# One layer of a hybrid decoder on one core: the last pair's forms moved into the second Strassen product, first loads on another queue, and result rows in another order

## The chip, the core and the metric

The kernel runs on one core of a Trainium2 chip. The core has a matrix engine (TensorE, PE in the profile, with its weight loads as PEld), a vector engine (VectorE, DVE), a scalar engine for activations (ScalarE, ACT), a general engine (GpSimd, POOL) and a queue engine that issues transfers (SyncE, SP). Sixteen DMA engines move data between the main memory and the on-chip memory (SBUF); matmul results go to eight banks of PSUM. All engines run on their own and wait for each other by semaphores. The metric is the device time of one execution in microseconds, here the median of three runs.

## The reference, cut to what matters

One layer for 1024 prompt positions and 8 single new positions, 1032 rows, width 1024, all in float32:

```
x = x + concat(gdn_heads(x), gating_heads(x)) @ w_out
x = x + square(relu(rms_norm(x, g_ff) @ w_up)) @ w_down        # 1024 -> 4096 -> 1024
x = x + (p @ w_ple) * sigmoid(rms_norm(x, g_ple) @ w_ple_gate) # p is 256 wide
y = rms_norm(x, g_final)
```

The change touches the second line's `w_down` product and how it begins, and the third and fourth lines.

## The kernel before

Float32 matmuls are made of three: every operand is split into a high part (a rounded copy, made by ScalarE) and a low part (the rest, made by VectorE), and hi*hi, lo*hi and hi*lo are summed in PSUM. Weights are split by `form` (lines 150 and 153), with four splits in flight.

Activations lie transposed, model columns on the partitions and rows on the free axis. The 1032 rows stand in four blocks of 256, 256, 260, 260; in the last stages they are two halves `nn` of two column blocks each, so a block number n has nn = n % 2 and column block n // 2. `q` numbers the 128-row output blocks of a half: q 0 and 1 lie in column block 0, q 2, 3 and 4 (the last with four rows) in column block 1.

Both products of the MLP use Strassen's scheme in the form with seven products, P1 to P7, in place of eight. In the first (lines 1167 to 1219) `p` counts 16 pairs of hidden units, t the two column blocks; the inputs' seven forms lie in `fb` and `fa` (fa serves P1, P4, P5; fb the others). Each pair's four results lie in one buffer `Q`; ScalarE copies P1's and P6's products out of PSUM, VectorE adds the others, ScalarE does relu and square in two passes, and `dforms` makes three subtractions on GpSimd (four of the seven forms that the second product needs) and writes three planes from Q and four from `tt` to `f_d` in main memory. For the last pair, relu and square of two planes are one VectorE instruction (line 1210), and its writes are issued by GpSimd. `up_rows` is a thread of extra work on the residual rows `x1_d` that takes one step per pair and column block.

In the second product (`down`, lines 1434 to 1507) four groups j of the hidden units each run the seven steps P1, P6, P7, P4, P2, P5, P3; n counts these 28 steps. Step n needs one plane of `f_d` in `raw` (`load_raw`), split into HC (`split_raw`: line 1347 on ScalarE, 1348 on VectorE, two halves each), and four forms of weights: P1 takes A11 alone, P6 the sums s1 = A21 + A22 and s2 = s1 - A11 (GpSimd, lines 1368 and 1369), P7 and P3 differences (line 1375). Each step has 96 matmuls on four parts p and two column blocks, and VectorE adds each result into one or two accumulators (lines 1463 and 1465): ACC holds C11, C12, C21, C22, and U2 and U3 lie beside it. `x1_old` loads the residual into an accumulator before the step that first adds to it. PE's and SP's orders are those of the program here; other engines' orders are chosen by the scheduler from priorities and readiness.

The on-chip memory is reused in place: xs, h1, A12, A22, A21, h0, A11 and raw take the space of fb, fa and Q. A22 lies under the end of fb, and A11, raw and h0 lie under fa. Later xt, wpl and pp take the space of h1, A12, A22, A21, h0 and A11.

In the last stage `gate_units` makes 8 x 4 gate products (24 matmuls each, lines 1658 to 1660) with the embedding product (`emb`, six matmuls), and `evg` multiplies by the row factor, takes a sigmoid, multiplies and adds to ACC (line 1649). Blocks 0 and 2 (half 0) come first for all m, then 1 and 3. `y_out` turns one 128-row block: two groups of four transposes (line 1626), a square with its sum for each (line 1627), the root of the mean square, two products (line 1636) and two writes (line 1637). The first half's `y_out` run beside the second half's gates; the second half's five come after the last gate. `pt` is the prompt's p, scaled on GpSimd (line 1504) and transposed by `p_in` (line 1579) at the beginning of the gates.

## Time and profile before

| | |
|---|---|
| median of 3 runs | 1414.2 us (1411.84, 1414.2, 1420.41) |
| profiled execution, its own time | 1418.24 us |
| its span, first to last instruction | 1416.5 us |
| PE busy | 1317.7 us, 93% of the span |
| DVE, POOL, ACT busy | 920.8, 696.9, 639.4 us |

The busy times say little by themselves: PE is nearly always busy, so what counts is where it stands, and for whom. The chain of work that ended last gives PE 72% of the span, DVE 9%, POOL 7%, ACT 4% and DMA 3%. PE's waits between 900 and 1270 us are 12.3 us for low parts of weights (DVE, line 153), 6.8 us for high parts (ACT, line 150) and 1.6 us for a copy of the row factor; from 1270 on they are 10.3 us, all for line 1636. The prediction's rows are from the timeline (start, length, engine, line, operation, out<-in, shape, count, and in brackets the idle time before it with what ended it) and from windows, whose columns it names.

### The profile page before, as it was taken

The page shows a single profiled execution, that of the slowest core. Times are in us where ns is not written, and L with a number is a line of the kernel's source. Part 1 is how long each engine was busy: PE and PEld are TensorE (multiplying, and loading weights), DVE is VectorE, ACT ScalarE, POOL GpSimd, SP SyncE. Part 2 cuts the span into 40 slices and gives each one's busy share as a digit, 9 for nine tenths or more (in the row PEclk, how much of TensorE's full clock was granted, in tenths as well). Part 3 has the DMA queues.
Part 4 walks back from the last instruction along what each step waited for, and adds up shares of the span by engine and source line. Part 5 has one row for each costly group of instructions (what it writes and reads, how often), then busy time and mean ns, then how long its engine had stood idle before and what let it go on. Part 6 is the DMA issues. An engine that isn't in the chain of part 4 may idle for free.

```text
span 1416.5 us, 26668 instructions
## 1 busy us (share of the span) xinstructions
PE 1317.7 (93%) x10189; PEld 1286.1 (91%) x10189; DVE 920.8 (65%) x1900; ACT 639.4 (45%) x1346; POOL 696.9 (49%) x720
## 2 busy tenths in 40 slices
PE   6979978999999799899999999789999999999995
PEld 5879968988989799899999999789999999899984
DVE  7745745455956856655545544678878878887664
ACT  6574645532232415555545445424333333545332
POOL 5300888746525404658856777640526136635110
PEclk9999988999999899999999999989999999999997
DMA  7334535545524831234545565776362524232221
GB/s 238 97 91 115 154 81 152 170 126 168 149 83 133 262 96 45 60 119 133 162 144 161 168 195 158 241 258 214 116 221 97 186 85 148 61 91 75 75 91 61
DMA packets 212076, 194.01 MB, mean 137 GB/s; under 512 B 20952, under 2 KB 181659, under 8 KB 211940
## 3 DMA queue, kind: packets, MB, share of 16 engines
q1 hardware_dynamic: 211436, 190.45, 43.6%
q8 instruction: 80, 1.31, 0.4%
q0 software_dynamic: 512, 1.85, 0.3%
q14 instruction: 48, 0.39, 0.1%
HBM read 131.75 MB, written 60.61 MB: 136 GB/s over the span
## 4 chain that ended last, share of the span: by engine, by line
PE 72%; DVE 9%; POOL 7%; ACT 4%; DMA 3%; issue 3%; SPq 1%; DVEq 0%; ACTq 0%; POOLq 0%
PE A L1184 9%; PE d L1457 7%; PE d L1458 7%; PE d L1456 7%; PE D L1184 7%; PE g L209 5%; PE g L211 5%; PE g L210 5%; PE B L1184 3%; PE C L1184 3%; PE g L1658 2%; POOL it L643 2%; POOL xinv L644 2%; PE g L1660 2%; PE g L1659 2%
## 5 line engine op out<-in xcount | busy, mean ns | idle before, releaser
L209 PE MATMUL g<-ra,whi 128*128 128x384 f32 (+3 forms) x800 | 275.4, 344 | 0.8 <-ACT ra L388 0.6
L1457 PE MATMUL d<-h,wlo 128*128 128x260 f32 (+1 forms) x896 | 256.7, 286 | 12.3 <-DVE wlo L153 12.3
L1456 PE MATMUL d<-h,whi 128*128 128x260 f32 (+1 forms) x896 | 254.4, 284 | 6.8 <-ACT whi L150 6.8
L211 PE MATMUL g<-ra,whi 128*128 128x384 f32 (+3 forms) x800 | 258.7, 323 | 0.8 <-POOL ra L389 0.4
L210 PE MATMUL g<-ra,wlo 128*128 128x384 f32 (+3 forms) x800 | 257.6, 322 | 0.0
L1458 PE MATMUL d<-h,whi 128*128 128x260 f32 (+1 forms) x896 | 256.0, 286 | 0.0
L1457 PEld LDWEIGHTS d<-h,wlo 128*128 128x128 f32 x896 | 171.4, 191 | 14.3 <-DVE wlo L153 14.0
L1456 PEld LDWEIGHTS d<-h,whi 128*128 128x128 f32 x896 | 172.1, 192 | 7.5 <-ACT whi L150 7.4
L1458 PEld LDWEIGHTS d<-h,whi 128*128 128x128 f32 x896 | 171.8, 192 | 0.0
L209 PEld LDWEIGHTS g<-ra,whi 128*128 128x128 f32 x800 | 156.6, 196 | 3.0 <-ACT ra L388 1.0
L211 PEld LDWEIGHTS g<-ra,whi 128*128 128x128 f32 x800 | 155.8, 195 | 2.5 <-POOL ra L389 1.7
L210 PEld LDWEIGHTS g<-ra,wlo 128*128 128x128 f32 x800 | 156.7, 196 | 0.7 <-DVE wlo L153 0.3
L153 DVE TENSOR_TENSOR wlo<-s,whi 128x512 fp32r<-128x512 f32 x96 | 73.5, 768 | 81.7 <-ACT whi L150 81.4
L153 DVE TENSOR_TENSOR wlo<-st,whi 128x512 fp32r<-128x512 f32 x94 | 75.8, 807 | 40.8 <-ACT whi L150 40.1
L1184 PE MATMUL A<-fb,whi 128*128 128x260 f32 (+1 forms) x512 | 95.6, 281 | 0.0
L643 POOL TENSOR_TENSOR it<-ainv,xinv 32x31 f32<-32x31 f32 (+15 forms) x124 | 75.3, 607 | 39.6 <-DMA ainv<-inv_d 30.3
L150 ACT CAST whi<-s 128x512 fp32r<-128x512 f32 x96 | 59.3, 618 | 76.1 <-PE D L1184 28.5
L1465 DVE TENSOR_TENSOR acc<-acc,d 128x256 f32<-128x256 f32 (+1 forms) x192 | 75.2, 414 | 20.9 <-PE d L1458 19.9
L1347 ACT CAST h<-raw 128x1024 fp32r<-128x1024 f32 (+1 forms) x56 | 58.6, 1055 | 65.2 <-DMA raw<-f_d 35.0
L150 ACT CAST whi<-st 128x512 fp32r<-128x512 f32 x96 | 59.1, 619 | 60.8 <-PE g L211 31.6
L1214 ACT ACTIVATE q<-q 128x512 f32<-128x512 f32 (+1 forms) x124 | 75.9, 631 | 22.0 <-DVE q L1207 16.1
L644 POOL TENSOR_TENSOR xinv<-xinv,it 32x31 f32<-32x31 f32 (+15 forms) x124 | 79.0, 637 | 9.6
(433 smaller groups left out, 3539.9 us busy)
## 6 DMA issues: line engine op xcount, KB each, us to landing
a<-in_w_down SPq DMA_DIRECT2D x16, 1024.0 KB
raw<-f_d SPq DMA_DIRECT2D x28, 520.0 KB
raw<-f_d SPq DMA_DIRECT2D x28, 512.0 KB
st<-in_w_in SPq DMA_DIRECT2D x24, 512.0 KB
ck<-ck_d SPq DMA_DIRECT2D x32, 320.0 KB
ra<-in_w_up SPq DMA_DIRECT2D x32, 256.0 KB
rb<-in_w_up SPq DMA_DIRECT2D x32, 256.0 KB
st<-in_w_ple_gate SPq DMA_DIRECT2D x16, 512.0 KB
```

Of the source, the lines that this page charges most:

```text
L150: S.copy(dst_hi, src)
L153: lo_eng.tensor_sub(dst_lo, src, f32(dst_hi))
L209: PE.matmul(ps[:, :w], lhsT=whi[k], rhs=xh, start=(k == 0), stop=False)
L210: PE.matmul(ps[:, :w], lhsT=wlo[k], rhs=xh, start=False, stop=False)
L211: PE.matmul(ps[:, :w], lhsT=whi[k], rhs=xl, start=False, stop=(k == nk - 1))
L643: G.tensor_mul(tv, a, x)
L644: G.tensor_sub(X[:, j + 1 :, :w], X[:, j + 1 :, :w], tv)
L1184: PE.matmul(ps, lhsT=a[:, k, :], rhs=x[:, c, k, :], start=(first and k == 0 and j == 0), stop=(k == 3 and j == 2), skip_group_check=True)
L1214: placed["act"] = S.activation(v, v, func).ins
L1456: PE.matmul(ps, lhsT=wh[:, k, :], rhs=xh[:, k, :], start=(k == 0), stop=False)
L1457: PE.matmul(ps, lhsT=wl[:, k, :], rhs=xh[:, k, :], start=False, stop=False)
L1458: PE.matmul(ps, lhsT=wh[:, k, :], rhs=xl[:, k, :], start=False, stop=(k == 3))
```

## The change

It has five parts. The last pair's relu and square of two planes and its subtractions leave the end of the first product: they are done in the second step of the second product (n = 1), the squares on ScalarE in two passes, the subtractions into space inside C22, and the four writes are issued by SP after step n = 2. So that they live that long, Q is allocated below fb and fa, and C22's residual is loaded after step 3, not 1. The first raw plane and A11 are loaded on ScalarE's queue, right after that engine's copy of the last pair's P6. `up_rows` takes the first column block of every second m together with the second, four steps fewer.

`pt` moves from the middle of the second product to its end, into space of A22, with its scaling.

In the last stage each half of a result block is multiplied by g_final unscaled, straight after its transposes, and its sum of squares is kept; one root serves several blocks (five in the first half, then three, then two), and the scaling by the root follows: 512 columns on ScalarE, 512 on GpSimd, and for the last two blocks the second half still by line 1636's instruction from PSUM. In the second half block 3 goes before block 1, and of m = 6 and 7 both of block 3 go before those of block 1, so that rows q 2, 3 and 4 are ready first; the table for the square root is loaded early by a dummy activation.

```diff
+        qst = ctx.enter_context(pool("qst"))
+        Q = qst.tile([P, 8 * 260], F32, name="q8")
         fx = ExitStack()
...
-                        S.copy(u2[t], ps)
+                        placed["u2", t] = S.copy(u2[t], ps).ins
...
                 if p == 15 and name == "P3":
-                    v = q[:, 0:4:3]
-                    V.scalar_tensor_tensor(v, in0=v, scalar=0.0, in1=v, op0=ALU.max, op1=ALU.mult)
+                    last.append((p, t, q))
...
+    def squared(v):
+        for func in (AF.Relu, AF.Square):
+            placed["act"] = S.activation(v, v, func).ins
+    def dforms_of(t, q, tt):
+        G.tensor_sub(tt[:, 1:4:2], q[:, 3:4].to_broadcast([P, 2, WT[t]]), q[:, 0:3:2])
+        G.tensor_sub(tt[:, 2], q[:, 2], tt[:, 1])
+        placed["pool"] = G.tensor_sub(tt[:, 0], q[:, 1], tt[:, 2]).ins
+    def dforms_out(p, t, q, tt):
+        w = WT[t]
         c0 = 1024 * t + w * (p % 4)
-        (G if p == 15 else SY).dma_start(f_d[p // 4, 0:3, ...], q[:, 0:3])
-        (G if p == 15 else SY).dma_start(f_d[p // 4, 3:7, ...], tt)
+        SY.dma_start(f_d[p // 4, 0:3, ...], q[:, 0:3])
+        SY.dma_start(f_d[p // 4, 3:7, ...], tt)
...
-                yield
+                if t or m % 2:
+                    yield
...
+    late = [C22.rearrange("p a b -> p (a b)")[:, 1024 * t : 1024 * t + 4 * WT[t]]... for t in range(2)]
...
+                if n:
+                    SY.dma_start(raw[:, c], f_d[j, DSTEPS[i][1], :, c])
+                else:
+                    with tc.issue_after(placed["u2", 0]), tc.high_priority(2 * PRI):
+                        S.dma_start(raw[:, c], f_d[j, DSTEPS[i][1], :, c])
...
+            if j or name != "A11":
+                SY.dma_start(dst, src[:, :, half * 512 : half * 512 + 512])
+            else:
+                with tc.issue_after(placed["u2", 0]), tc.high_priority(2 * PRI):
+                    S.dma_start(dst, src[:, :, half * 512 : half * 512 + 512])
...
+                if n == 1 and p < 2:
+                    _, t, q = last[p]
+                    with tc.issue_after(placed["cast", 1]):
+                        squared(q[:, 0:4:3])
+                    with tc.issue_after(placed["sum"]):
+                        dforms_of(t, q, late[t])
...
+            elif n == 2:
+                for p, t, q in last:
+                    dforms_out(p, t, q, late[t])
+            elif n == 3:
                 x1_old(C22, 1, 1)
-            elif n == 10:
-                SY.dma_start(pt, p_prompt[0, 0].rearrange("(c p) d -> p c d", p=P))
...
+    with tc.high_priority(3 * PRI):
+        SY.dma_start(pt, p_prompt[0, 0].rearrange("(c p) d -> p c d", p=P))
...
+    yot = [Q[:, :1024], Q[:, 1024:2048]] + [ty.tile([P, D], F32, name=f"yo{i}") for i in range(3)]
...
+    def y_half(nn, q, a, keep=False):
+        r = rows_of(q)
+        ps = pss.tile([P, 512], F32, tag="s2", name="yT")
+        for j in range(4):
+            PE.transpose(ps[:r, j * P : j * P + P], ACC[:, a, nn, j, q * P : q * P + r], ident)
+        junk = tp.tile([P, 512], F32, tag="jk", bufs=1, name="jk")
+        S.activation(junk[:r], ps[:r], AF.Square, accum_out=sty[:r, nn, q, a : a + 1])
+        b = slice(512 * a, 512 * a + 512)
+        if not keep:
+            V.tensor_mul(yos[nn, q][:r, b], ps[:r], gfb[:r, b])
+        return ps
+    def y_roots(nn, q0, q1, fast=False):
+        v = rsy[:, nn, q0:q1]
+        V.tensor_add(v, sty[:, nn, q0:q1, 0], sty[:, nn, q0:q1, 1])
+        V.scalar_tensor_tensor(v, in0=v, scalar=1.0 / D, in1=ems[:, nn, q0:q1], op0=ALU.mult, op1=ALU.add)
+        (rsqrt_act if fast else rsqrt)(tp, v, v, f"ry{nn}{q0}")
+    def y_end(nn, q, ps=None):
...
+        S.activation(yo[:r, :512], yo[:r, :512], AF.Copy, scale=s)
+        if ps is None:
+            G.tensor_scalar_mul(yo[:r, 512:], yo[:r, 512:], s)
+        else:
+            V.scalar_tensor_tensor(yo[:r, 512:], in0=ps[:r], scalar=s, in1=gfb[:r, 512:], op0=ALU.mult, op1=ALU.mult)
+        for b in (slice(0, 512), slice(512, 1024)):
             SY.dma_start(y[:, b], yo[:r, b])
...
-        weave(gate_units((1, 3), True))
+        weave(gate_units([(m, n) for m in range(6) for n in (3, 1)], True))
+        spawn(first_halves())
+        weave(gate_units([(6, 3), (7, 3)], True))
+        spawn(second_out(), 2.5)
+        weave(gate_units([(6, 1), (7, 1)], True))
+        with tc.issue_after(placed["sig"]):
+            S.activation(rsy[:, 1, 0:1], ones[:, 0:1], AF.Sqrt)
         drain()
-        for q in range(5):
-            for _ in y_out(1, q):
-                pass
+        pa = [y_half(1, q, 1, True) for q in range(2)]
+        y_roots(1, 0, 2, True)
+        for q in range(2):
+            y_end(1, q, pa[q])
```

`first_halves` runs `y_half(1, q, 0)` for q = 2, 3, 4, 0, 1; `second_out` runs `y_half(1, q, 1)` for q = 2, 3, 4, one root for the three, and their `y_end`.

More of the change, by code (lines that the diff above doesn't have):

```diff
@@ L1318, in trunk_step_kernel @@
     U2, U3 = (dac.tile([P, 4, 516], F32, name=f"u{i}") for i in (2, 3))
+    late = [C22.rearrange("p a b -> p (a b)")[:, 1024 * t : 1024 * t + 4 * WT[t]].rearrange("p (a b) -> p a b", a=4)
+            for t in range(2)]
     INTO = {"P1": (U2, C11), "P6": (U2,), "P7": (U3,), "P4": (C21,), "P2": (C11,), "P5": (C12, C22), "P3": (C12,)}
@@ L1339, in load_raw @@
             for c in (slice(0, 1024), slice(1024, 2064)):
-                SY.dma_start(raw[:, c], f_d[j, DSTEPS[i][1], :, c])
+                if n:
[3 more added lines that the diff above has]
+                        S.dma_start(raw[:, c], f_d[j, DSTEPS[i][1], :, c])
     def split_raw(n):
@@ L1346, in split_raw @@
                 for c in (slice(0, 1024), slice(1024, 2064)):
-                    S.copy(hi[:, c], raw[:, c])
+                    placed["cast", n] = S.copy(hi[:, c], raw[:, c]).ins
                     V.tensor_sub(lo[:, c], raw[:, c], f32(hi[:, c]))
@@ L1368, in down_forms @@
                             G.tensor_add(s1[:, p], a_of("A21", p), a_of("A22", p))
-                            G.tensor_sub(s2[:, p], s1[:, p], a_of("A11", p))
+                            placed["sum"] = G.tensor_sub(s2[:, p], s1[:, p], a_of("A11", p)).ins
                             f = s2[:, p]
@@ L1604, in emb @@
         return ps
-    def root(tok, tag, fast):
-        (rsqrt_act if fast else rsqrt)(tp, tok, tok, tag)
     def rows(nn):
@@ L1614, in rows @@
         arrived("r", nn)
[L1616 to L1636 removed]
+    yos = {(nn, q): yot[q] for nn in range(2) for q in range(5)}
@@ L1637, in y_out, with gate_units @@
             SY.dma_start(y[:, b], yo[:r, b])
-    def gate_units(blocks, last):
-        for m in range(KD):
+    had = {}
+    def gate_units(turns, last):
+        for m, n in turns:
             def evg(ps, n, m=m):
@@ L1649, in evg @@
                 (V if last and m > 5 else G).tensor_add(xv, xv, t)
[L1651 to L1667 removed]
+            if m not in had:
+                had[m] = next_w()
+            ws = had[m]
+            w = WT[n // 2]
+            ps = gps[0].tile([P, 512], F32, tag="g", name="g")[:, :w]
+            for k in (4, 5, 6, 7, 0, 1, 2, 3):
+                wh, wl = (h[:, k % 4, :] for h in ws[k // 4])
+                xh, xl = (h[:, k % 4, TOFF[n // 2] : TOFF[n // 2] + w] for h in XS[k // 4, n % 2])
+                PE.matmul(ps, lhsT=wh, rhs=xh, start=(k == 4), stop=False)
+                PE.matmul(ps, lhsT=wl, rhs=xh, start=False, stop=False)
+                PE.matmul(ps, lhsT=wh, rhs=xl, start=False, stop=(k == 3))
+                if k == 3:
+                    with tc.high_priority(PRI):
+                        if there >= {("p", n % 2), ("r", n % 2)}:
+                            evg(ps, n)
+                        else:
+                            held.append((n, lambda ps=ps, n=n, evg=evg: evg(ps, n)))
+                yield 3 * w * 0.000455
     held, there = [], {("r", 0)}
@@ L1696, in first_out, with first_halves, second_out @@
         for q in range(5):
-            yield from y_out(0, q)
+            for a in range(2):
+                y_half(0, q, a)
+                yield YT
+        y_roots(0, 0, 5)
+        for q in range(5):
+            y_end(0, q)
+    def first_halves():
+        for q in (2, 3, 4, 0, 1):
+            y_half(1, q, 0)
+            yield YT
+    def second_out():
+        for q in (2, 3, 4):
+            y_half(1, q, 1)
+            yield YT
+        y_roots(1, 2, 5)
+        for q in (2, 3, 4):
+            y_end(1, q)
     with tc.manual_schedule(engines={mybir.EngineType.PE}):
```

85 lines of the change are left out of this document (27 added, 58 removed).

## The prediction

> **What bounds the kernel now.** I read the spans first, then the waits of TensorE, then stage windows, then the timelines of the two stretches that the change touches: the hand-over from the first Strassen product (line 1184) to the second (lines 1456 to 1458), and the end.
>
> ```profile
> core 0: 1416.5 us, clock 0.964
> ```
> ```profile
> 913.00:921.50 8.50, 0.57 (x3) 0.19 (x1) 8.24 (x6) 2.52 (x5) 8.29 (x8) 0.67 1.05 386
> 921.50:926.00 4.50, 4.45 (x20) 4.45 (x21) 4.50 (x2) 0.00 (x0) 4.16 (x5) 0.50 1.05 399
> ```
> ```profile
> 935.00:940.00 5.00, 0.32 (x3) 0.11 (x1) 5.00 (x10) 0.62 (x1) 1.79 (x2) 0.98 0.14 32
> 940.00:945.00 5.00, 4.84 (x29) 4.84 (x30) 3.35 (x6) 1.57 (x2) 0.00 (x0) 0.68 0.88 300
> ```
> The columns are the stretch and its length, then busy time (and instructions) of PE, PEld, DVE, ACT, POOL, then granted clock, DMA share, GB/s. Elsewhere PE is full; here it stands for most of 13.5 us, while DVE is full, and in 921.5:926 it runs at half clock (0.50).
>
> ```profile
> 921.55 0.58 PE L1457 MATMUL d<-h,wlo 128*128 128x256 f32 x1 [5.52 <-DVE wlo L153]
> ...
> 940.16 0.58 PE L1457 MATMUL d<-h,wlo 128*128 128x256 f32 x1 [4.84 <-DVE wlo L153]
> ```
> ```profile
> 913.23 0.43 DVE L1207 TENSOR_TENSOR q<-u,D 128x260 f32<-128x260 f32 x1 [0.30 <-PE D L1184]
> 913.69 1.29 DVE L1210 SCALAR_TENSOR_TENSOR q<-q 128x520 f32<-128x520 f32 x1
> 914.90 5.45 DVE L1348 TENSOR_TENSOR h<-raw,h 128x1024 fp32r<-128x1024 f32 x2
> 920.28 9.48 DVE L153 TENSOR_TENSOR wlo<-a,whi 128x512 fp32r<-128x512 f32 x4
> ...
> 937.14 2.37 DVE L1348 TENSOR_TENSOR h<-raw,h 128x1024 fp32r<-128x1024 f32 x2
> 939.43 1.88 DVE L153 TENSOR_TENSOR wlo<-s,whi 128x512 fp32r<-128x512 f32 x3
> ```
> The same DVE work takes 5.45 us at 914.9 and 2.37 at 937.1 (two halves of the low part), 2.37 and 0.63 us each (the weights' low part). The slow ones stand where POOL is full (8.29 of 8.50), the fast ones where it is idle. So the hand-over is bound by DVE slowed beside POOL, and what POOL does first is the last pair's forms (lines 1226 to 1231); the sums for the second step come behind them:
>
> ```profile
> 923.54 5.07 POOL L1368 TENSOR_TENSOR s<-a,a 128x512 f32<-128x512 f32 x4
> 930.49 1.32 POOL L1375 TENSOR_TENSOR sd<-a,a 128x512 f32<-128x512 f32 x1 [1.88 <-issue]
> 931.75 5.03 POOL L1369 TENSOR_TENSOR s<-s,a 128x512 f32<-128x512 f32 x4
> 949.55 1.30 POOL L1375 TENSOR_TENSOR sd<-a,a 128x512 f32<-128x512 f32 x1 [12.76 <-DVE wlo L153]
> ```
> The end: five blocks of result rows after the last gate matmul (1393.63 + 0.28 = 1393.9) take to 1416.5, 22.6 us, a chain of transposes, squares, a root and a product for each block, with two buffers.
>
> ```profile
> 1393.63 0.28 PE L1603 MATMUL em<-pp,wpl 128*128 128x260 f32 x1
> ```
> ```profile
> 1394.60 0.43 DVE L1649 TENSOR_TENSOR acc<-acc,t 128x260 f32<-128x260 f32 x1
> 1395.82 0.16 DVE L1630 TENSOR_TENSOR st<-st 128x1 f32<-128x1 f32 x1 [0.79 <-ACT yo L1627]
> 1396.01 0.16 DVE L1631 SCALAR_TENSOR_TENSOR st<-st,ems 128x1 f32<-128x1 f32 x1
> ```
> ```profile
> 1396.38 1.28 ACT L261 ACT_TABLE_LOAD   x1
> ```
> ```profile
> 1412.63 0.73 DVE L1636 SCALAR_TENSOR_TENSOR yo<-yT,st,gfb 4x512 f32<-4x512 f32 x1
> 1412.73 0.93 SPq L1637 DMA_DIRECT2D out<-yo  x2
> ```
>
> **Part 1: hand-over.** Removed from it: the two products of line 1210 on DVE, six POOL subtractions, four POOL DMAs. Moved before it: the loads of raw and A11.
>
> ```profile
> 903.28 0.37 ACT L1198 COPY u<-A 128x256 f32<-128x256 f32 x1 [0.74 <-PE A L1184]
> ```
> ```profile
> 905.69 0.94 SPq L1340 DMA_DIRECT2D raw<-f_d  x2
> 906.68 6.91 SPq L1355 DMA_DIRECT2D a<-in_w_down  x3
> ```
> ```profile
> 911.00 1.05 ACT L1347 CAST h<-raw 128x1024 fp32r<-128x1024 f32 x1 [0.80 <-DMA raw<-f_d]
> 912.28 1.06 ACT L1347 CAST h<-raw 128x1040 fp32r<-128x1040 f32 x1 [0.23 <-DMA raw<-f_d]
> 914.97 2.18 ACT L150 CAST whi<-a 128x512 fp32r<-128x512 f32 x4 [1.63 <-DMA a<-in_w_down]
> ```
> ScalarE may issue them from 903.7 (the copy's end), 2.0 us ahead of SP's 905.69. No ACT-issued DMA is in this trace; three at SP's 0.47 us each are 1.4 us, which holds that pair's second copy until about 905.2; its reader also waits for the next step's matmuls, so I count nothing for that. A11, cast at 914.97 now, comes about 912.9, so its cast (0.55) is done by 913.5. The last product's result is read at 913.23 + 0.43 = 913.7; then DVE has one half of the low part (1.2, alone; the other is done before) and the first weight (0.63): **first step running at 915.5** instead of 921.55, and at full clock, the gap being 2.3 us. Its 96 matmuls at 0.12 (below) end at 927.0.
>
> The second step needs A22, which still waits for the last matmul (its place lies under the operand that this reads), so it lands at 918 to 921 (5.3 us from issue to cast for raw, 8 for A11): 919. POOL, free now, sums four (5.07): 924.1, a difference and a step between (1.3 + 1.3): 926.7, cast and low part (0.55 and 0.63 to 2.37): 927.9 to 929.6. DVE between 915.5 and there: three weights 1.9, 16 evacuations at 0.43 = 6.9, the next low part 2.4 to 5.45, the first weight 0.63 to 2.37: 11.8 to 16.6, so 927.3 to 932.1. I take 929.5, nearer the slow end, as POOL's sums do run beside it. Before, this was 940.16, and 29 matmuls in 4.84 us instead of 3.5 make it 941.5 in effect. **Gain 12.0**, ends 14.5 (927.0) and 8.1 (932.1 and the restart again, 1.3).
>
> The forms come back in the second step: on POOL two 512 wide at 1.3 and four 256 wide at some 0.7, 5.4 us beside DVE. In the 11.5 us of that step DVE has 3.4 of evacuations and 4.3 of splits alone, and if half of the splits slow 2.3-fold, 10.5: it fits. I take +0.5, ends 0 and +2. The four squares on ScalarE (busy 1.57 of 5 us in 940:945) and the four writes on SP, issued behind the third step's loads, lie beside matmuls: 0; without that cover the writes (seven planes of 128 x 516 fp32, 1.85 MB, at 399 GB/s) would cost 4.6 us of DMA.
>
> On the DMA move, the row first: 1.05 of the DMA engines' time is taken in 913:921.5. The Trainium skill ("DMA: Bandwidth & Descriptors", Issuing engines are not separate DMA queues) says that another issuer saves only issue time, and (Queues, rings and completion order) that each engine takes turns between queues. By that, A11 on ScalarE's queue shares with A21 on SP's, which stood behind it: 0.5 MB more ahead of it, 1.3 us at 386 GB/s; the sum would be 1.3 us worse. No run here shows two such queues yet.
>
> **Part 2: the end.** Eight groups of four transposes now run before the last gate matmul.
>
> ```profile
> 1333.86 0.28 PE L1660 MATMUL g<-xt,whi 128*128 128x260 f32 x1
> 1333.98 0.60 PE L1626 MATMUL yT<-ident,acc 128*128 128x128 f32 x4
> 1334.33 0.36 PE L1658 MATMUL g<-xt,whi 128*128 128x260 f32 x1
> ```
> ```profile
> 1360.80 0.36 PE L1601 MATMUL em<-pp,wpl 128*128 128x256 f32 x1 [2.37 <-DVE yo L1636]
> ```
> A matmul takes 0.12 (1333.86 to 1333.98); a group adds 0.35: 8 x 0.35 = +2.8. The banks are freed by a product that waits for no root, so the stall of 2.37 goes: -2.4. Net **+0.4**, ends -1 and +2.4.
>
> From the last gate matmul (0): the add ends at 1.1. ScalarE: sigmoid to 0.2, table 1.28 and its dummy root: 1.7; the squares of block 4 and of blocks 0 and 1 (0.8 each, a square and its read-out): 2.5, 3.3, 4.1. DVE: the root of three blocks, 13 small instructions at 0.19 (1395.82 to 1396.01): 2.5 to 5.0. Then POOL scales three halves of 512 columns, and its price is the scaling of pt, 256 columns wide:
>
> ```profile
> L1504 POOL TENSOR_SCALAR pt<-pt,mst 128x256 f32<-128x256 f32 x8 | 7.8, 993 | 19.9 <-PE d L1458 19.9
> ```
> Twice 0.99 less a start is 1.8: 3 x 1.8 = 5.4, to 10.4. The last write to the end takes 3.1 now (1413.36 to 1416.5): **13.5**. The other path, blocks 0 and 1: squares 4.1, sum 0.4, root 0.6, four ops 0.8, up to 1.1 behind the other root, two products 1.5: 7.4 to 8.5, with 3.1 10.5 to 11.6. So POOL ends last; it is the price I trust least. **Gain 22.6 - 13.5 = 9.1**, ends 12.1 (POOL hidden) and 5.6 (outputs of blocks 0 and 1 issued behind it, 1.9, and POOL slowed by DVE).
>
> **Part 3: pt.** Its load and 7.8 us of POOL scaling move from the middle to after the second product's last load.
>
> ```profile
> 1231.10 1.47 SPq L1340 DMA_DIRECT2D raw<-f_d  x2
> ```
> It can issue at 1232.6, when its place (A22's) is long free, and is first read at 1266; POOL has gaps there, but DVE is slowed. +0.5, ends 0 and +3. The other edits (fewer steps for x1, C22 loaded two steps later, buffers) are hidden by the same matmul stretches: 0, and 1 us each if not.
>
> **Sum**: -12.0 + 0.5 + 0.4 - 9.1 + 0.5 = **-19.7 us**. The profiled execution took 1418.24 us for its span of 1416.5, so it would take 1398.5; it lies 4.0 above the median of 1414.2, and from the median this is **1394.5**.
>
> **Rivals.**
> Half of the hand-over: DVE stays the bound, as POOL's sums and then the forms run beside every split (5.45 against 2.37). The second step at 935 is 5.5 later than my 929.5, with a restart at half clock 1.3 more and 0.5 in the steps behind: 7.3 lost, 1401.8, within 1%. For it: DVE 5.00 of 5.00 even in 935:940. Against: there POOL is busy 1.79 only.
>
> Cold restarts: PE's clock was 0.50 after 5.52 us idle and 0.68 after 4.84. Should both gaps left (2.3 and 2.5) outgrow that, each costs 1.3 to 2.2: 1394.5 + 3.5 = 1398. The Trainium skill ("TensorE: Matmul & The Clock Gate", Part 1) puts the limit at an idle window of about 3.4 us; the trace agrees with gaps on its far side only.
>
> Slower: SP takes its queue in order, so the late writes hold the fifth loads behind them until POOL has the forms. The fifth step's operand must be issued by about 962 (its step starts at 929.5 + 4 x 11.5 = 975.5, less 13 for a load of 5.3, casts of 2.1 and splits of 5.45); past that each us costs one, and from 982 on all is lost. If the forms stood behind POOL's later differences and ended at 995, 33 are lost: 1427.5. Against: POOL idles 12.76 us before 949.55.
>
> The change doesn't do what it says (POOL's order leaves the forms first): only part 2, 1406.
>
> **How the numbers follow.** A measurement here can tell about 1%, so faster is under 1400.1, slower above 1428.3. The forecast has 0.73, cold restarts in it; half a hand-over has 0.16 and none 0.05, both within 1%; the held queue has 0.06, half of it within 1% and half past it: 0.73, 0.24, 0.03. Best ends: 14.5 + 12.1 + 1 = 27.6, 1386.6; the bad side reaches to the no-hand-over case, 1406. Range 1386 to 1406.
>
> **What would show it.** Right: the first step's second matmul within 2.5 us of the last of line 1184; the second step 10 to 14 us earlier; the clock at 1.00 there; the splits at 1.2 and 0.65; 13 to 14 us after the last gate matmul, POOL's scaling last in the chain. Wrong: DVE full and PE waiting for low parts past 935; a wait for pt before the gate; outputs held behind POOL by 4 us or more; SP waiting for the late forms.

## The result, and the profile after

The changed kernel takes 1404.8 us (median of 20 runs, 1399.52 to 1412.71) against 1412.3 us for the kernel before on the same chips (20 runs, 1405.05 to 1420.41): ratio 0.995, interval 0.9935 to 0.9966. It gains 7.5 us where 19.7 were forecast. The time lies inside the range given, 1386 to 1406, near its upper end, and within 1% of no change, which had a chance of 0.24.

The profiled execution of the changed kernel:

```profile
core 0: 1400.9 us, clock 0.971
```

This span is 15.6 us below the one shown of before, but 8.5 us of that lie ahead of the last matmul of the first product (at 913.2 before, 904.7 after), in code that the change leaves alone. Two executions of one kernel differ by as much. So I count from that matmul on, where the traces differ by 7.1 us, close to the 7.5 of the medians. The starts of the second product's steps (96 matmuls each) and the first and last matmul of the gate stage divide that stretch:

| us | before | after | difference | forecast |
|---|---|---|---|---|
| first product's last matmul to third step | 39.7 | 33.1 | -6.6 | -11.5 |
| third step to the end of the second product | 310.0 | 310.4 | +0.4 | 0 |
| gate stage, to the last embedding matmul | 131.0 | 138.6 | +7.6 | +0.9 |
| from there to the end | 22.6 | 14.2 | -8.4 | -9.1 |
| all, before rounding | 503.3 | 496.2 | -7.1 | -19.7 |

**Hand-over.** TensorE's timeline (start, length, engine, line, then the idle time before it and what ended it) and the windows (stretch and length, busy time of PE, PEld, DVE, ACT, POOL, granted clock, DMA share, GB/s):

```profile
911.71 0.58 PE L1479 MATMUL d<-h,whi 128*128 128x256 f32 x1 [7.05 <-ACT h L1365]
```
```profile
908.00:911.70 3.70, 0.00 (x0) 0.00 (x0) 3.60 (x6) 2.91 (x4) 0.08 (x1) 0.50 1.04 391
911.70:917.50 5.80, 5.33 (x23) 5.03 (x24) 1.97 (x3) 0.45 (x1) 4.35 (x4) 0.50 0.92 315
917.50:930.00 12.50, 12.50 (x106) 12.50 (x106) 11.86 (x18) 8.66 (x13) 12.50 (x9) 1.00 0.64 213
```

The two waits for low halves of weights, 5.52 and 4.84 us, are gone. In their place stands one wait of 7.05 us for the cast of raw, and then 5.8 us at half clock. ScalarE's timeline tells why raw is late:

```profile
898.92 2.75 ACT L1224 ACTIVATE q<-q 128x512 f32<-128x512 f32 x4 [2.31 <-DVE q L1203]
901.04 0.45 ACTq L1378 DMA_DIRECT2D a<-in_w_down  x1
901.52 0.99 ACTq L1358 DMA_DIRECT2D raw<-f_d  x2
906.63 2.18 ACT L150 CAST whi<-a 128x512 fp32r<-128x512 f32 x4 [4.96 <-DMA a<-in_w_down]
908.99 1.06 ACT L1365 CAST h<-raw 128x1040 fp32r<-128x1040 f32 x1 [0.19 <-DMA raw<-f_d]
910.61 1.04 ACT L1365 CAST h<-raw 128x1024 fp32r<-128x1024 f32 x1 [0.56 <-DMA raw<-f_d]
```

The three loads stand behind the four activations of the last pair's other planes, and are issued at 901.04 to 902.5, 3 us before the last matmul. SyncE issued raw 7.5 us before it in the kernel before. A11 (a<-in_w_down, 1 MB) also goes out ahead of raw here, where SyncE had sent raw first, and it lands first: its cast begins at 906.63, raw's two at 908.99 and 910.61. From 902 to 908 us ScalarE's queue (q10) moved 1.99 of the 2.01 MB:

```profile
q10 hardware_dynamic: 771, 1.99, 95.9%
```

So raw is late for two reasons, its issue and the megabyte ahead of it. Until the first of these loads moved data the DMA engines stood idle, as their row for 892 to 912 us in slices of 0.5 us shows (4, 0 and 0 GB/s from 900.5 to 902):

```profile
GB/s 10 0 0 12 332 324 357 343 324 229 195 314 377 401 406 406 189 4 0 0 147 111 197 365 410 410 436 381 415 373 378 389 385 401 401 406 401 375 381 348
```

**The load of pt.** SyncE, TensorE and GpSimd at the start of the gate stage:

```profile
1216.95 1.47 SPq L1355 DMA_DIRECT2D raw<-f_d  x2
1241.92 0.38 SPq L1569 DMA_DIRECT2D st<-in_w_ple_gate  x1
1242.35 1.70 SPq L1594 DMA_DIRECT2D yo<-in_w_ple  x2
1244.09 0.67 SPq L1599 DMA_DIRECT2D pt<-in_p_sample  x2
1244.80 0.35 SPq L1600 DMA_DIRECT2D gfb<-in_g_final  x1
1246.26 0.40 SPq L1569 DMA_DIRECT2D st<-in_w_ple_gate  x1
1246.70 0.99 SPq L1548 DMA_DIRECT2D pt<-in_p_prompt  x1
```
```profile
1256.59 6.33 POOL L1552 TENSOR_SCALAR pt<-pt,mst 128x256 f32<-128x256 f32 x7 [3.10 <-DMA pt<-in_p_prompt]
```
```profile
1257.57 0.48 PE L1615 MATMUL pT<-ident,pt 128*128 128x128 f32 x1 [7.28 <-POOL pt L1552]
```

SyncE had issued the last raw load by 1218.4 and then stood for 23.5 us at a weight load whose buffer was not free. Everything emitted behind the second product came after that, and pt (line 1548) last but for the weights of later tiles, at 1246.7, 28.3 us behind the last raw load, where the prediction had it straight behind. Why the scheduler placed it so late, in spite of its high priority, no run shows. It landed at 1256.6, and TensorE waited 7.28 us for it, and then ran at half clock again.

**The end.** The last embedding matmul is at 1386.44 + 0.28, and then:

```profile
1393.56 4.63 POOL L1680 TENSOR_SCALAR yo<-yo,rsy 128x512 f32<-128x512 f32 x3 [22.38 <-DVE rsy L254]
```
```profile
1392.66 1.80 SPq L1685 DMA_DIRECT2D out<-q  x4
1394.55 3.94 SPq L1685 DMA_DIRECT2D out<-yo  x6
```

GpSimd scales last, as forecast, three at 1.54 us each (1.8 were taken), but it begins 6.8 us after the last embedding matmul instead of 5.0. The DMA engines are full from the first write on, which the prediction had not counted (the window's last columns are DMA share and GB/s):

```profile
1393.50:1398.50 5.00, 0.00 (x0) 0.00 (x0) 0.00 (x0) 1.94 (x3) 4.63 (x3) 0.50 1.04 389
```

### The profile page after: what moved, and what is told of

It reads as the page before. It is cut to its first block, busy times and chain, and to the rows that moved or that the text cites. A ratio compares the mean times of both kernels' runs of the same rounds, so it can differ in the third digit from the quotient of the medians.

```text
span 1400.9 us, 26613 instructions
## 1 busy us (share of the span) xinstructions
PE 1307.6 (93%) x10189; PEld 1276.7 (91%) x10189; DVE 899.3 (64%) x1836; ACT 646.4 (46%) x1357; POOL 707.4 (50%) x724
## 3 DMA queue, kind: packets, MB, share of 16 engines
q10 hardware_dynamic: 816, 2.11, 0.4%
## 4 chain that ended last, share of the span: by engine, by line
PE 69%; POOL 10%; DVE 9%; issue 4%; ACT 4%; DMA 3%; SPq 0%; POOLq 0%; ACTq 0%; DVEq 0%
PE A L1184 9%; PE D L1184 6%; PE d L1480 6%; PE d L1481 6%; PE d L1479 6%; PE g L209 5%; PE g L211 5%; PE g L210 5%; PE B L1184 3%; PE C L1184 3%; POOL xinv L644 3%; POOL it L643 3%; PE g L1709 2%; DVE wlo L153 2%; PE g L1710 2%
## 5 line engine op out<-in xcount | busy, mean ns | idle before, releaser
L209 PEld LDWEIGHTS g<-ra,whi 128*128 128x128 f32 x800 | 155.0, 194 | 3.0 <-ACT ra L388 1.0
L211 PEld LDWEIGHTS g<-ra,whi 128*128 128x128 f32 x800 | 154.0, 192 | 2.5 <-POOL ra L389 1.6
L1224 ACT ACTIVATE q<-q 128x520 f32<-128x520 f32 (+1 forms) x128 | 78.3, 631 | 22.1 <-DVE q L1207 16.1
L1365 ACT CAST h<-raw 128x1040 fp32r<-128x1040 f32 (+1 forms) x56 | 58.6, 1056 | 60.5 <-DMA raw<-f_d 29.5
L1488 DVE TENSOR_TENSOR acc<-acc,d 128x256 f32<-128x256 f32 x192 | 75.2, 414 | 16.5 <-PE d L1481 15.5
```

Of the source, the lines that this page charges most:

```text
L209: PE.matmul(ps[:, :w], lhsT=whi[k], rhs=xh, start=(k == 0), stop=False)
L211: PE.matmul(ps[:, :w], lhsT=whi[k], rhs=xl, start=False, stop=(k == nk - 1))
L1224: placed["act"] = S.activation(v, v, func).ins
```

## The experiments

Each trace is divided as above, in us. "Gap" is TensorE's wait between the first product's last matmul and the second product's first one, "third" is the time from the first product's last matmul to the third step, "last" the length of the second product's last step, "gate" the gate stage to the last embedding matmul, "end" the rest. Ratios are against runs of the kernel before on the same chip.

| run | ratio (interval) | gap | third | last | gate | end |
|---|---|---|---|---|---|---|
| before | 1 | 2.45 | 39.7 | 12.7 | 131.0 | 22.6 |
| after | 0.995 (0.9935 to 0.9966) | 7.05 | 33.1 | 12.7 | 138.6 | 14.2 |
| e_raw_sp | 0.9974 (0.9954 to 0.9994) | 0.37 | 39.1 | 12.7 | 138.1 | 14.4 |
| e_pt_a22 | 0.9936 (0.9915 to 0.9957) | 7.02 | 33.4 | 19.4 | 128.6 | 13.9 |
| e_both | 0.9935 (0.9912 to 0.9959) | 0.35 | 35.9 | 16.6 | 129.8 | 14.4 |
| e_tail | 0.9988 (0.9973 to 1.0003) | 2.78 | 40.5 | 19.5 | 131.4 | 14.7 |
| f_pt2 | 0.988 (0.9856 to 0.9904) | 6.98 | 33.7 | 12.8 | 129.3 | 14.1 |
| f_forms3 | 0.9893 (0.9871 to 0.9915) | 6.90 | 33.6 | 12.8 | 129.3 | 14.5 |
| f_sp_forms3 | 0.9906 (0.9883 to 0.9928) | 0.54 | 31.6 | 12.8 | 128.9 | 14.3 |
| f_g_forms3 | 0.9872 (0.9849 to 0.9896) | 2.61 | 30.4 | 12.8 | 129.4 | 14.6 |
| h_tail | 0.9946 (0.9926 to 0.9966) | 2.37 | 40.4 | 12.8 | 129.8 | 14.8 |
| h_g_forms1 | 0.9864 (0.9841 to 0.9888) | 2.61 | 30.2 | 12.8 | 129.3 | 14.7 |
| h_best | 0.9872 (0.9854 to 0.989) | 2.62 | 30.4 | 12.8 | 129.3 | 14.7 |
| i_aligned | 0.985 (0.9816 to 0.9883) | 2.61 | 30.3 | 12.7 | 129.5 | 14.7 |

My theory after the first reading: two places cost the missing 12 us, each a matter of which queue issues a load and behind what. The rivals: the loads couldn't have come sooner, or what TensorE gains there is lost a step later.

### The first loads back on SyncE's queue (e_raw_sp)

```diff
-                if n:
-                    SY.dma_start(raw[:, c], f_d[j, DSTEPS[i][1], :, c])
-                else:
-                    with tc.issue_after(placed["u2", 0]), tc.high_priority(2 * PRI):
-                        S.dma_start(raw[:, c], f_d[j, DSTEPS[i][1], :, c])
+                SY.dma_start(raw[:, c], f_d[j, DSTEPS[i][1], :, c])
...
-            if j or name != "A11":
-                SY.dma_start(dst, src[:, :, half * 512 : half * 512 + 512])
-            else:
-                with tc.issue_after(placed["u2", 0]), tc.high_priority(2 * PRI):
-                    S.dma_start(dst, src[:, :, half * 512 : half * 512 + 512])
+            SY.dma_start(dst, src[:, :, half * 512 : half * 512 + 512])
```

> The changed kernel with one part undone: the first step's three loads (raw's two halves and A11) go back to SyncE's queue, raw first, ahead of A21 and A22. Theory (the loads were late because ScalarE's queue issues them behind four activations, at 901.0 to 902.5, 3 us before the first product's end, and because they then share the DMA engines with A21): SyncE is through with the older writes at 894.2, so raw is issued some 10 us before the end of the first product instead of 3, the 7.05 us gap ahead of the second product's first matmul shrinks to under 3 us and the half clock after it goes; 5 to 8 us less than the changed kernel, about 1398. Rival (raw cannot come sooner, its place or its transfer sets the time, or what is won returns as a stall in the second step because A21 and A22 now come after 2 MB): raw's casts stay within 2 us of where they were or a stall of 4 us or more appears at the second step; within 2 us of the changed kernel, about 1405.

The edit also puts raw ahead of A11. The first half of the theory held: raw was issued at 894.52, 10.4 us before the last matmul, and the gap fell to 0.37 us. The rest went to the rival: two waits for VectorE came instead, the third step began at 39.1 us, as late as in the kernel before, and the run took 1408.96 us. From TensorE's, VectorE's and GpSimd's timelines:

```profile
909.41 0.58 PE L1472 MATMUL d<-h,wlo 128*128 128x256 f32 x1 [3.72 <-DVE wlo L153]
```
```profile
930.55 0.58 PE L1472 MATMUL d<-h,wlo 128*128 128x256 f32 x1 [6.99 <-DVE wlo L153]
```
```profile
921.28 6.13 DVE L1362 TENSOR_TENSOR h<-raw,h 128x1024 fp32r<-128x1024 f32 x1
...
928.00 1.23 DVE L1362 TENSOR_TENSOR h<-raw,h 128x1040 fp32r<-128x1040 f32 x1
```
```profile
915.99 5.06 POOL L1384 TENSOR_TENSOR s<-s,a 128x512 f32<-128x512 f32 x4
921.02 2.56 POOL L1228 TENSOR_TENSOR acc<-q 128x512 f32<-128x512 f32 x2
923.55 1.41 POOL L1229 TENSOR_TENSOR acc<-q,acc 128x256 f32<-128x256 f32 x2
924.93 1.40 POOL L1230 TENSOR_TENSOR acc<-q,acc 128x256 f32<-128x256 f32 x2
```

A22's lateness, which the rival named, is not the reason: GpSimd had the sums by 921.05. A subtraction that takes 1.23 us alone took 6.13 us while GpSimd ran the last pair's moved forms, and the weights' low halves stood behind it.

### The load of pt as early as before (e_pt_a22), and both (e_both)

```diff
+    AC = {"A22": xst.tile([P, 2064], F32, name="a22")}
+    pt = AC["A22"][:, :2048].rearrange("p (c d) -> p c d", c=NU)
...
+            elif n == 25:
+                SY.dma_start(pt, p_prompt[0, 0].rearrange("(c p) d -> p c d", p=P))
+                for nn in range(2):
+                    for q in range(4):
+                        x = pt[:, pcol(nn, q), :]
+                        G.tensor_scalar_mul(x, x, mst[:, nn, q : q + 1])
```

> The changed kernel with pt's load as early as in the kernel before: pt takes A22's buffer, its load is issued by SyncE in step 25 of the second product's 28, behind that step's raw loads, and scaled by POOL there. Theory (pt's 7.28 us wait ahead of the first transposes and the half clock behind it come from pt being last in SyncE's queue, 4.8 us behind the weights that waited for a buffer): the wait goes, and from the gate's first matmul to the last embedding matmul it takes 128 to 129 us instead of 137.0; 8 to 9 us less than the changed kernel, about 1396. Rival (something else is as late at that place, such as the row sums or the weights' casts, and the wait only changes its name): that stretch stays above 134 us and the time within 3 us of the changed kernel.

> The two edits together: first loads on SyncE's queue, raw first, and pt in A22's buffer. Theory (the two stalls are separate places on TensorE's path): the gains add up, 13 to 17 us less than the changed kernel, about 1390. Rival (TensorE's path is not what sets the end in one of the two stretches): no more than the larger of the two gains, 8 to 9 us, about 1396.

The gate stage fell from 138.6 to 128.6 us, as the theory had it, but the last step of the second product rose from 12.7 to 19.4. GpSimd had been given pt's scaling ahead of the last row sums, and TensorE waited for those:

```profile
1231.21 11.17 POOL L1537 TENSOR_SCALAR a<-a,mst 128x256 f32<-128x256 f32 x8 [1.95 <-PE d L1482]
1242.35 1.26 POOL L1419 TENSOR_TENSOR ss<-ss,sq 128x516 f32<-128x516 f32 x1
1243.58 1.26 POOL L1399 TENSOR_TENSOR sd<-a,s 128x512 f32<-128x512 f32 x1
1244.80 1.27 POOL L1419 TENSOR_TENSOR ss<-ss,sq 128x516 f32<-128x516 f32 x1
```
```profile
1246.12 1.02 PE L1432 MATMUL ms<-ones,ss 128*128 128x1 f32 x4 [3.48 <-POOL ss L1419]
```
```profile
1246.00:1252.00 6.00, 5.88 (x28) 5.83 (x29) 4.79 (x16) 1.76 (x3) 2.62 (x3) 0.50 0.03 5
```

3.48 us of wait and these 6 us at half clock make up most of the 6.7 us. The run took 1402.54 us instead of the 1396 expected. With both edits the same happened (16.6), so e_both says nothing on whether the gains add up; it is inconclusive.

### The end alone (e_tail, h_tail)

The last pair's forms, their writes, the first loads and the steps of `up_rows` as in the kernel before; pt in A22's buffer, with e_pt_a22's scaling in e_tail and f_pt2's (next section) in h_tail.

```diff
                 if p == 15 and name == "P3":
-                    last.append((p, t, q))
+                    v = q[:, 0:4:3]
+                    V.scalar_tensor_tensor(v, in0=v, scalar=0.0, in1=v, op0=ALU.max, op1=ALU.mult)
...
-                if p < 15 and name == "P3":
+                if name == "P3":
...
-        SY.dma_start(f_d[p // 4, 0:3, :, c0 : c0 + w].rearrange("f p c -> p f c"), q[:, 0:3])
+        (G if p == 15 else SY).dma_start(f_d[p // 4, 0:3, :, c0 : c0 + w].rearrange("f p c -> p f c"), q[:, 0:3])
```

> Only the end of the change: the last pair's forms, its writes on POOL's queue and the first loads on SyncE's queue are as in the kernel before, pt is loaded early into A22's buffer, and the third part (unscaled columns, joint roots, later block first) stays. Theory: the hand-over from the first product to the second costs what it cost before (8.3 us to the first step, a stall of about 5 us in the second), and the end has the gain that the traces show, 22.6 to 14.2 us after the last embedding matmul, and 131 to about 128.5 us from the gate's start to there; 11 us less than the kernel before, about 1401. Rival (the later block first and the joint roots pay for themselves elsewhere in the gate stage): 8 us or less against the kernel before, 1404 or more.

> The end of the change alone, again, now with pt's scaling behind the row sums as in the second pt run (the first try at this paid a wait of 3.46 us for the row sums and a half clock after it, 19.5 us for the last step instead of 12). The last pair's forms, their writes and the first loads are as in the kernel before. Theory (the end is worth what the prediction said of it, 8.4 to 9.1 us behind the last embedding matmul, and the two waits in the gate stage that go with the joint roots another 2 to 3): from the gate's first matmul to the last embedding matmul 127 to 128 us, then 14 to 15 us, the hand-over as before; 10 to 12 us less than the kernel before, about 1402. Rival (the end gives some of it back): less than 7 us.

e_tail paid the row sums' wait as well. h_tail gives the end alone: from the first product on 496.0 us, 7.3 us less than before (end -7.8, gate -1.2, hand-over and middle +1.7), and 6.5 us by the medians (1405.71 against 1412.18). The end's own 7.8 us are there; the sum of 10 to 12 that I expected is not, and the rival's bound, less than 7, lies between the two measures.

### pt's scaling behind the row sums (f_pt2)

```diff
+            elif n == 25:
+                SY.dma_start(pt, p_prompt[0, 0].rearrange("(c p) d -> p c d", p=P))
+            elif n == 26:
+                for nn in range(2):
+                    for q in range(4):
+                        x = pt[:, pcol(nn, q), :]
+                        with tc.issue_after(placed["ss"]), tc.issue_after(placed["sd"]):
+                            G.tensor_scalar_mul(x, x, mst[:, nn, q : q + 1])
```

> The changed kernel with pt in A22's buffer and loaded in step 25, as in the run with pt alone, but scaled by POOL only behind the last row sum and the last form of the second product. In the first pt run the gate stage lost 9.0 us and the last step of the second product took 19.5 us instead of 12.6, behind a 3.48 us wait for POOL's row sums, which stood behind pt's scaling. Theory (that wait and the half clock after it are the place where the gain went): the last step returns to 12.6 us, the gate stage stays at 128 us; 8 to 9 us less than the changed kernel, about 1396. Rival (the last step is long for another reason, such as the load of pt against raw's last loads): the last step stays over 17 us, and the time at about 1402.

The theory held: last step 12.8, gate 129.3, 1395.5 us. The scaling now lies where GpSimd is idle, and TensorE's longest wait near it is 0.91 us:

```profile
1248.89 7.71 POOL L1539 TENSOR_SCALAR a<-a,mst 128x256 f32<-128x256 f32 x8
```
```profile
1257.53 0.36 PE L1711 MATMUL g<-xs,whi 128*128 128x256 f32 x1 [0.91 <-DVE acc L1489]
```

So the late pt cost the change some 9 us, and no longer wait is left there.

### Where the moved forms run, and who issues the first loads (f_forms3, f_sp_forms3, f_g_forms3, h_g_forms1)

All four are f_pt2 with one or two edits: the last pair's squares and forms in the fourth step (f_forms3), then also the first loads on SyncE's queue (f_sp_forms3) or on GpSimd's (f_g_forms3); h_g_forms1 has the loads on GpSimd's queue and the forms where the change put them.

```diff
-                if n == 1 and p < 2:
+                if n == 3 and p < 2:
...
-                    with tc.issue_after(placed["cast", 1]):
+                    with tc.issue_after(placed["cast", 4]):
...
-                        S.dma_start(raw[:, c], f_d[j, DSTEPS[i][1], :, c])
+                        G.dma_start(raw[:, c], f_d[j, DSTEPS[i][1], :, c])
...
-                    S.dma_start(dst, src[:, :, half * 512 : half * 512 + 512])
+                    G.dma_start(dst, src[:, :, half * 512 : half * 512 + 512])
```

> As the run before it, and the last pair's squares and forms moved two steps further, to the second product's fourth step (their write and the load into their place one step later). Theory (in the changed kernel TensorE no longer waits in the first three steps except for its first operands, so POOL's time there is covered): the third step begins as late after the first product as in the changed kernel, 33.2 us; time equal to the run before it within 1 us. Rival (POOL's forms slow VectorE's subtractions, and with them TensorE, even there): 2 us or more less.

> As the run before it, and the first loads on SyncE's queue with raw first. In the run with these loads on SyncE alone, the first gap fell from 7.05 to 0.37 us, and 3.72 and 6.99 us of waits for VectorE's low halves came in the first and second step; one of VectorE's subtractions, of 1.23 us elsewhere, took 6.13 us there and ended within 1.1 us of POOL's last moved form. Theory (POOL's moved forms hold VectorE up, and so the second step): the second wait falls below 2 us and the third step begins 28 to 31 us after the first product instead of 39.2; 2 to 5 us less than the run of this call with pt alone. Rival (VectorE is simply full, or A22 is too late, whatever POOL does): the second wait stays at 4 us or more, and the time within 2 us of that run or above it.

> As the run with the forms in the fourth step, and the first loads on POOL's queue, where nothing stands ahead of them from 10.9 us before the first product's end, beside A21 on SyncE's. Theory (on ScalarE's queue the loads are late by the activations ahead of them): A11 and raw are issued about 10 us before the end, raw's casts are done before the end and the gap ahead of the first step falls from 7.05 to 2 us or less, the third step begins at 28 us or earlier; 4 to 6 us less than the run with the forms in the fourth step alone. Rival (three megabytes at once are late however they are issued): a gap of 4 us or more.

> The run with the first loads on POOL's queue, with the last pair's forms where the changed kernel has them, in the second step, instead of the fourth. Theory (POOL's forms hold VectorE's subtractions up when TensorE waits for them): a subtraction of 2 us or more beside them, a wait of 2 to 5 us in the second or third step, the third step beginning 32 us or later after the first product instead of 30.4; 2 to 4 us more than the run with the forms in the fourth step. Rival (in this order VectorE is ahead and can stand it, as in the changed kernel, where the move of the forms from the second to the fourth step changed nothing): third step within 1 us, time the same.

f_forms3 changed nothing (third step 33.6 against 33.7, and the traces 0.3 us apart from the first product on; the medians, 1397.35 and 1395.5 us, differ by more than the 1 us expected, in the way of noise): where TensorE had already waited for its first operands, the forms are covered. With the loads on SyncE's queue they weren't. Moving them took VectorE's first subtraction of the same pair from 6.13 us to 1.22, the second wait from 6.99 to 1.41 us, and the third step from 39.1 to 31.6, just outside the 28 to 31 expected. Those are against e_raw_sp; e_both, which has pt in the same place as this run, began its third step at 35.9, so the move is worth 4.3 to 7.5 us. From VectorE's and TensorE's timelines of f_sp_forms3:

```profile
922.13 1.22 DVE L1363 TENSOR_TENSOR h<-raw,h 128x1024 fp32r<-128x1024 f32 x1
```
```profile
925.82 0.39 PE L1473 MATMUL d<-h,wlo 128*128 128x256 f32 x1 [1.41 <-DVE wlo L153]
```

On time, too, it missed its expectation: 1398.92 us, where f_pt2 took 1395.5, although its trace is 1.0 us shorter from the first product on. A difference that small is below what the medians tell.

On GpSimd's queue the loads were issued at 894.4, 11 us before the last matmul, and A11's casts ran straight behind the activations:

```profile
894.41 1.00 POOL L1379 DMA_DIRECT2D a<-in_w_down  x1
895.40 1.07 POOL L1359 DMA_DIRECT2D raw<-f_d  x2
```
```profile
902.29 1.65 ACT L150 CAST whi<-a 128x512 fp32r<-128x512 f32 x3
905.41 0.62 ACT L150 CAST whi<-a 128x512 fp32r<-128x512 f32 x1 [1.47 <-PE D L1184]
905.94 2.00 ACT L1366 CAST h<-raw 128x1040 fp32r<-128x1040 f32 x2
```
```profile
907.99 0.38 PE L1480 MATMUL d<-h,whi 128*128 128x256 f32 x1 [2.61 <-ACT h L1366]
910.59 0.58 PE L1482 MATMUL d<-h,whi 128*128 128x256 f32 x1 [2.10 <-DVE h L1367]
```

The third step began at 30.4 us instead of 33.6: 3.2 us of the hand-over's shortfall were the issue behind the activations. The medians give 2.4 us (1394.94 against 1397.35). That is less than the 4 to 6 I expected, as 2.61 and 2.10 us of waits are left, for raw's cast and for its low half, which VectorE takes behind the four weights. In h_g_forms1 the forms are back in the second step and cost nothing (30.2); the expected wait didn't come. So among these runs the forms' slowing of VectorE shows on TensorE's path only in the order of loads that e_raw_sp has.

### GpSimd's share of the end (h_best)

```diff
-            G.tensor_scalar_mul(yo[:r, 512:], yo[:r, 512:], s)
+            (V if (nn, q) == (1, 3) else G).tensor_scalar_mul(yo[:r, 512:], yo[:r, 512:], s)
...
-        y_roots(1, 2, 5)
+        with tc.high_priority(PRI):
+            y_roots(1, 2, 5)
```

> The run with the first loads on POOL's queue and the forms in the fourth step, and two edits of the end: of the three tiles that POOL scales last, VectorE takes the second, and the three joint roots are put ahead of VectorE's two output tiles. Theory (POOL's three scalings of 1.54 us each, from 1382.9 to 1387.5 of 1390.7, are what ends last): POOL is done 2.5 to 3 us earlier against the last embedding matmul, and the end takes 12 us instead of 14.6; about 1392.5. Rival (the output writes on SyncE's queue, ten of 0.4 to 0.7 us each and their landing, set the end): 14 us or more.

The rival was right: the end stayed at 14.7 us.

```profile
1383.57 3.26 POOL L1682 TENSOR_SCALAR yo<-yo,rsy 128x512 f32<-128x512 f32 x2 [20.98 <-DVE rsy L254]
```
```profile
1384.17 1.30 SPq L1687 DMA_DIRECT2D out<-q  x3
1385.56 3.38 SPq L1687 DMA_DIRECT2D out<-yo  x6
1388.99 0.35 SPq L1687 DMA_DIRECT2D out<-q  x1
```

GpSimd is done at 1386.83, yet SyncE issues until 1389.34, with a tile that was ready early in last place, and the span ends 3.6 us behind that. The DMA engines were full meanwhile:

```profile
1385.00:1389.50 4.50, 0.00 (x0) 0.00 (x0) 0.41 (x1) 1.59 (x3) 1.83 (x2) 0.50 1.04 393
```

The ten writes are 2.11 MB, 5.4 us at 393 GB/s, and the first is issued 6.0 us after the last embedding matmul. With the last landing that fills the end, so I take the writes' own time for what holds it. No run made them fewer or earlier, so this is argued and not shown.

### Where the right-hand operands lie (i_aligned)

The middle steps of the second product last the same to 0.01 us within a run, but not between kernels: 11.38 (odd) and 11.48 us (even) before, 11.40 and 11.53 after, 11.52 for both wherever pt shares A22's buffer. The four buffers of raw's halves lie at other addresses in each. This run is h_g_forms1, instruction for instruction, with these buffers, and A22's ahead of them, 64 bytes longer, which puts each at a multiple of 128 bytes of its partition; whatever lies behind them moves too.

```diff
-    HC = [None, [dl.tile([P, 2064], F32R, name=f"h1{i}") for i in range(2)]]
+    HC = [None, [dl.tile([P, 2080], F32R, name=f"h1{i}") for i in range(2)]]
```

> The run with the first loads on POOL's queue and the forms in the second step, instruction for instruction, but the four buffers of TensorE's right-hand operands in the second product are 64 bytes longer, so that all of them begin at a multiple of 128 bytes of a partition. The steps in the middle of the second product take 11.40 (odd) and 11.53 us (even) in the changed kernel, 11.38 and 11.48 before, and 11.52 for both in every run where pt shares A22's buffer, each to 0.01 us, at a granted clock of 1.00; the high halves (two of three matmuls) begin 0, 64, 128, 64 and 64 bytes past a multiple of 128 or 256 there. Theory (a matmul whose operand begins 64 bytes past a multiple of 128 is slower): 11.25 to 11.40 us for all steps, 3 to 7 us less than that run, 1387 to 1391. Rival (the addresses are not it, but what else moves on the chip): 11.52 us still, and the time of that run, 1393.7.

Odd and even steps both took 11.41 us, 0.11 less: with the same instructions, where the buffers lie counts. The size was overestimated: from the third step to the last it is 1.6 us (298.9 to 297.3), and the time, 1392.33 against 1393.72, can't tell that from nothing. It is the fastest kernel of the study by its median, 0.985 (0.9816 to 0.9883) of the kernel before, where the change has 0.995 (0.9935 to 0.9966).

## Why the prediction was wrong

- **What bounds the kernel: right.** TensorE's path has its slack in the hand-over, the gate stage's start and the end, and the stretch between differs by 0.4 us.
- **Part 1, the step that failed: "ScalarE may issue them from 903.7 (the copy's end), 2.0 us ahead of SP's 905.69".** I took the earliest point that the code allows for the point where the queue gets there. ScalarE's queue had four activations of the same pair in between, and raw went 4.4 us later against the last matmul than on SyncE (3.1 instead of 7.5 us ahead of it). I also had raw ahead of A11 on the queue, and A11 went first: 1 MB, an estimated 2.6 us at the 399 GB/s of 904 to 908 us. No run had raw first on ScalarE's or GpSimd's queue, so what the order alone cost stays open. The second step began at 21.7 us after the last matmul instead of 16.3; f_g_forms3 brought it to 18.9 and the third step 3.2 us forward, to 30.4 where 28.2 was forecast. The rest, some 2 us, I put down to what f_g_forms3 still shows, raw's cast and VectorE's order (I had one half of raw's low part ahead of the first weight, and there the four weights come first); no run took these away.
- **Part 1, the forms: right in size, for a different reason.** +0.5 was counted and h_g_forms1 against f_g_forms3 shows nothing (30.2 and 30.4). But the argument "it fits" held only because TensorE was late or VectorE ahead. In e_raw_sp the same forms took 4.9 us of VectorE's time.
- **Part 1, the shared queues: not tested in the changed kernel.** The 1.3 us by the Trainium skill's rule ("DMA: Bandwidth & Descriptors", Queues, rings and completion order) would need A21 and A11 under way together. A21 was through at about 900.5, before A11 was issued: the DMA row shows nothing moving then. In f_g_forms3 two queues did move together: from 898 to 906 us GpSimd's carried 2.11 MB and SyncE's 1.05 MB, 394 GB/s in all.
- **Part 2: right in size, in part by luck.** 14.2 us against 13.5, and GpSimd does scale last. But it began 1.8 us later than forecast and was faster for each tile, and it doesn't set the end alone: h_best took a tile of the three from it and the end stayed. The sum had no term for the writes, which fill the DMA engines for over 5 us. In the gate stage the forecast of +0.4 was too careful: the stall of 2.37 us is gone, and so are waits of 1.6 and 0.8 us, so that h_tail and f_pt2 are 1.2 and 1.7 us below the kernel before.
- **Part 3, the second step that failed: "It can issue at 1232.6, when its place (A22's) is long free ... +0.5, ends 0 and +3".** The place was free, but the queue wasn't looked at. pt had left the order written out by hand for the second product, and behind that SyncE first stood at a weight load for 23.5 us and then took everything else first. It cost 7.28 us of wait and a half clock; f_pt2 gives back some 9 us. It lies far outside the ends I gave, which were priced by GpSimd's scaling alone. The prediction's own sign of being wrong, a wait for pt before the gate, is what came; it had no price there.
- **The rivals.** Half a hand-over had 0.16 and is nearest to what came (the second step 21.8 us after the last matmul there, 21.7 measured), but by luck: VectorE was not its cause. Cold restarts came in both places, behind 7.05 and 7.28 us of waits, and the first cost some 2.6 us (23 matmuls took 5.33 us, at 0.12 each they take 2.8), more than the 1.3 to 2.2 named. SyncE held by the late writes didn't happen.
- **The sum.** With pt early and the first loads on a queue that was free, h_g_forms1 takes 1393.72 us, 0.9864 (0.9841 to 0.9888) of the kernel before: 18.5 us less, where 19.7 were forecast. The change's idea was worth about what the prediction said, though not in the same places: by its trace the hand-over gives 9.5 us (11.5 forecast), the end 8.0 (9.1), the gate stage 1.8 (a loss of 0.9 was forecast), and the second product's middle takes 1.7 more (0), part of it by where the buffers lie.

## What to carry to other kernels

A DMA is issued when its queue reaches it, so a load that moves to another engine or out of a hand-written order is to be placed by what stands ahead of it there: the last instructions of that engine before the point, and any buffer that the queue will wait for. In the changed kernel the first cost 4.4 us on raw's issue, the second 28.3 us on pt's. A wait that goes hands TensorE to the next one: e_raw_sp took 6.7 us off the gap and lost more than that in the next two waits, so follow the path to a mark past the whole stretch (here the third step) before counting a gain. An engine's program order matters as much as its load: pt's scaling cost 6.7 us ahead of two row sums (e_pt_a22) and nothing behind them (f_pt2).

## What the runs showed of the hardware that I had not expected

**VectorE behind GpSimd, all or half.** In e_raw_sp VectorE's subtraction from two operands in SBUF began 0.26 us after GpSimd's run of six instructions and ended after all of them (6.13 us; GpSimd's two of 512 columns took 1.28 us each, its other four 0.70, undisturbed). In e_both the same instructions began 0.05 us apart and both were slowed (GpSimd's to 1.77 us each):

```profile
921.25 2.33 DVE L1363 TENSOR_TENSOR h<-raw,h 128x1024 fp32r<-128x1024 f32 x1
```
```profile
921.20 3.53 POOL L1228 TENSOR_TENSOR acc<-q 128x512 f32<-128x512 f32 x2
```

VectorE began the weights' low halves at 929.82 in the one and at 926.41 in the other, and the third step came 3.2 us apart (39.1 and 35.9), in two kernels with the same instructions there. The Trainium skill ("SBUF — State Buffer", Who interferes with whom) says that of such a pair the later one is blocked until the first has finished, and that the order of issue decides; the 2.33 us agree with a block of one instruction (1.28 us, and 1.22 for the subtraction alone), but 6.13 us is a block through all six. What decides between the two was not tested.

**Two short gaps, and half the clock.** In f_g_forms3 no gap was longer than 2.61 us, and two matmuls ran between 2.61 and 2.10, yet the clock went to half:

```profile
909.00:910.50 1.50, 0.00 (x0) 0.00 (x0) 1.50 (x2) 0.00 (x0) 0.00 (x0) 0.50 1.06 397
910.50:915.00 4.50, 4.41 (x20) 4.42 (x21) 0.79 (x3) 0.00 (x0) 3.83 (x4) 0.50 1.07 398
```

The Trainium skill ("TensorE: Matmul & The Clock Gate", What's actually happening) has a window of 3413 ns that runs freely. The trace agrees if, as I read it, gaps shorter than the window add up when they fall together into one; no run was made to test this.

**Operand addresses.** At a granted clock of 1.00, 96 matmuls took 11.41 us in i_aligned and 11.52 in h_g_forms1, which differ in where the buffers of the right-hand operands begin, 1% in the second product's steady part. Which of the two halves' addresses counts was not separated.
